# Sixteen keys in 128 rows: zero-filled last blocks in a two-layer attention and retention kernel

## The chip, the cores and the metric

The kernel runs on one core of a Trainium2 chip. The metric is the device time of one execution in microseconds (us). Three runs of the kernel before took 1307.19, 1303.7 and 1307.78 us; their median is 1307.19 us. One further execution was taken with the hardware profiler: it took 1307.29 us, and its trace spans 1305.5 us.

## What is computed

The model is a trunk of two layers. Each layer normalises its input, projects it once, splits the columns into a softmax attention with forget gates (8 heads of 64, called FoX here) and a retention (4 heads of 128), joins both, projects back, and runs a gated feed-forward network. 16 learned "meta" tokens stand ahead of the 512 real tokens, so the sequence has 528 positions: four blocks of 128 and a last one of 16.

```python
def fox_attention(q, k, v, logf):
    ...
    def attend(q_blk, c_q, q_pos, k_, v_, c_k, k_pos):
        s = jnp.einsum('bhqd,bhkd->bhqk', q_blk, k_).astype(jnp.float32) * scale
        s = s + c_q[..., :, None] - c_k[..., None, :]
        s = jnp.where(k_pos[None, :] <= q_pos[:, None], s, -jnp.inf)
        p = jax.nn.softmax(s, axis=-1)
        return jnp.einsum('bhqk,bhkd->bhqd', p.astype(v_.dtype), v_)
...
def retention_chunkwise(q, k, v):
    """o_t = sum_{s<=t} gamma_h^(t-s) (q_t.k_s) v_s."""
...
def hybrid_layer(h, ...):
    xn = rmsnorm(h, attn_norm_g)
    proj = jnp.einsum('bld,dc->blc', xn, w_in)
    ...
    mix = jnp.concatenate([fox_out, ret_out], axis=-1)
    h = h + jnp.einsum('blc,cd->bld', mix, w_out)
    ...
    return h + jnp.einsum('blf,fd->bld', ff, w_down)
```

## The kernel before

Activations lie transposed, features on the 128 partitions and the 528 positions along the free dimension. Every product is made in float32r with both operands split into a high and a low part (`split`, L119: ScalarE copies the high part, VectorE subtracts it to get the low part), so that a product is two or three matmuls. In the trace such tiles come in pairs: `pth` and `ptl`, `rsh` and `rsl`, `rvh` and `rvl`, `whi` and `wlo`.

A layer has two stages. In the attention stage (the pool `att`, entered by `enter_att`, L81) the dense projections of w_in and w_out run on TensorE (L191), and the steps of the attentions are placed between them. In the feed-forward stage (the pool `ffn`) there are only dense products and forms of them (L803, L938). The two pools lie over each other: a tile of a pool waits for the tile of the earlier pool on whose addresses it lies.

The order of TensorE is written out by hand: `layer` builds a list of steps, `merge` (L215) puts each attention step at a given place between the dense steps, and `tc.manual_schedule` (L1121) keeps TensorE in that order. The other engines' order is left to a scheduler. Weights arrive by DMAs of SyncE's queue (L135); ScalarE copies their high part (`whi`, L167), and VectorE or GpSimd subtracts the low part (`wlo`, L168).

The attention steps that the change touches:

- `transpose_into` (L369) transposes column blocks of a tile on TensorE, up to four into one PSUM bank. It takes `parts`, the number of rows of its source, and `last`, the number of columns in a last block that stands alone. Its matmul (L378) has the data as the stationary operand, which a weight load brings into the array, and an identity matrix (`idt`) as the moving one.
- FoX (`fox_steps`, L425; two heads share a step list, s = 0 and 1). `values` (L431) transposes V in five blocks at `KOFF`, the last of 16 columns, and splits it into `vv`. `scores` (L447) makes the logits of one query block and writes the exponentials to `p_tiles[b]`, or, for the 16 meta queries, to one of two tiles of 16 rows (`pm_tiles`). `turn` (L497) transposes them into `pth` and `ptl`, [128, 5, 528]; for meta queries the source has 16 rows (`nq`). `product` (L507) multiplies by the values: five key blocks, a high and a low matmul for each, all in one PSUM bank. The fifth block has `KLEN[4]` = 16 rows of both operands and only 16 queries.
- Retention (`ret_steps`, L592). `values` (L598) transposes `vr`, subtracts the mean over each head's 128 columns and splits into `rvh` and `rvl`. `scores` (L617) makes the decayed products of key blocks; the blocks 2, 3 and 4 share a pair of tiles `rsh` and `rsl`, and the part of block 4, 16 rows by 16 columns, is split by itself (L651). `product` (L654) takes three matmuls for a block (high by high, high by low, low by high), for the fifth block with 16 rows.
- Layer 0 also computes the 16 meta queries, layer 1 doesn't. So a run has 16 FoX products (8 heads, 2 layers), 8 retention products, and 8 transposes of meta queries.

The rows of a matmul are the partitions of both its operands, over which it sums. The lines at which the fifth block gets its 16 rows:

```python
rows = last if j0 + len(grp) == len(offs) and len(grp) == 1 else 128
nc.tensor.transpose(ps[0:rows, 128 * j:128 * j + parts], src[:, o:o + rows], idt[0:parts, 0:parts])
...
kn = KLEN[j]
nc.tensor.matmul(po[:, c0:SEQ], v[0:kn, j, :], pp[0:kn, j, META + c0:T],
                 start=(j == 0 and i == 0), stop=(j == 4 and i == 1))
```

Of the kernel before, what the change touches and what calls it, by code (L numbers as in the profile page):

```python
# [17 lines left out]
SEQ = 512  # L18
# [20 lines left out]
def hybrid_kernel(ctx, tc, x_t, w_in, w_fl, w_out, w_gate, w_up, w_down, vecs, b_fg, rope, decay, mask, ident, out_t):  # L39
# [24 lines left out]
    onec = const.tile([128, 1], F32, name="onec")  # L64
    nc.vector.memset(onec, 1.0)

    p_tiles, pm_tiles, vt_tiles, low_keys = [], [], [], []
    rot = {"pm": 0, "vt": 0}


    phase = {}
# [9 lines left out]
    def enter_att(l):  # L81
        enter("att")
        low_keys[:] = [phase["att"].tile([128, T], F32R, name=f"kl{s}") for s in range(2)]
        for s, t in enumerate(low_keys):
            (nc.gpsimd if l else nc.vector).memset(t[64 * (1 - s):64 * (2 - s)].bitcast(F32), 0.0)
        for lst, n, shape in ((p_tiles, NBLK, [128, TP]), (pm_tiles, 2, [META, 128]), (vt_tiles, 1, [128, T])):
            lst[:] = [phase["att"].tile(shape, F32, name=f"pd{shape[1]}_{n}_{i}") for i in range(n)]

            for i, t in enumerate(lst):
                if lst is not vt_tiles:  # L90
                    z0 = META + 128 * (i + 1) if lst is p_tiles else META
                    (nc.gpsimd if l else nc.vector).memset(t[:, z0:z0 + 128 - META], 0.0)

    def take(lst, key):
        t = lst[rot[key] % len(lst)]
# [273 lines left out]
    def transpose_into(src, offs, parts=128, last=128):  # L369


        out = []
        for j0 in range(0, len(offs), 4):
            grp = offs[j0:j0 + 4]
            ps = psum_a()
            rows = last if j0 + len(grp) == len(offs) and len(grp) == 1 else 128
            for j, o in enumerate(grp):
                nc.tensor.transpose(ps[0:rows, 128 * j:128 * j + parts], src[:, o:o + rows], idt[0:parts, 0:parts])  # L378
            out.append((j0, len(grp), rows, ps[0:rows, 0:128 * len(grp)].rearrange("p (j q) -> p j q", j=len(grp))))
        return out  # L380

    def fox_dense(l, g, ly, real, st):
# [28 lines left out]
                st["k"].append((kh, kl))  # L411

        def v_done(ps):
            vt = take(vt_tiles, "vt")
# [10 lines left out]
    def fox_steps(g, st, ly, real):  # L425
# [21 lines left out]
        def scores(s, b):  # L447
# [11 lines left out]
            for c0, c1 in segs:  # L459
                sc = psum_a()  # L460
                for i, kk in enumerate(st["k"][s]):
                    nc.tensor.matmul(sc[0:nq, 0:c1 - c0], st["q"][s][:, q0:q0 + nq], kk[:, c0:c1],  # L462
                                     start=(i == 0), stop=(i == 1))
                if c1 == nk:
                    diag = sc[0:nq, c1 - c0 - nq:c1 - c0]
                    nc.vector.tensor_add(diag, diag, msk[0:nq, 0:nq])
                nm = tmp.tile([128, 1], F32, name="nmax", tag="nmax", bufs=6)
                nc.vector.tensor_tensor_reduce(pt[:, c0:c1], sc[0:nq, 0:c1 - c0], bc[0:nq, c0:c1],  # L468
                                               -1.0, 3.0e38, ALU.add, ALU.min, nm[0:nq])
                mins.append(nm)  # L470
            nmax = mins[0]
# [8 lines left out]
            pr = pt[:, 0:nk]  # L480
# [16 lines left out]
        def turn(s, b):  # L497
            nq, nk, q0 = span(b)
            if b == blocks[0]:
                st["pt"] = (at("pth", shape=(128, 5, T)), at("ptl", shape=(128, 5, T)))  # L500
            pth, ptl = st["pt"]
            if (s, b) == todo[-2]:
                normalise()
            for j0, n, _, p3 in transpose_into(info[s, b], [128 * j for j in range(b + 2)], nq):
                split(pth[:, j0:j0 + n, q0:q0 + nq], ptl[:, j0:j0 + n, q0:q0 + nq], p3[:, :, 0:nq])

        def product(s):  # L507
# [10 lines left out]
            po = psum_a()  # L518
            for j in range(5):
                c0 = max(0, KOFF[j] - META)  # L520
                kn = KLEN[j]
                for i, pp in enumerate(pt):
                    nc.tensor.matmul(po[:, c0:SEQ], v[0:kn, j, :], pp[0:kn, j, META + c0:T],  # L523
                                     start=(j == 0 and i == 0), stop=(j == 4 and i == 1))
            nc.scalar.copy(ol[a0:a1, META:T], po[b0:b1, :])
            nc.vector.tensor_add(mt[a0:a1, META:T], po[a0:a1, :], ol[a0:a1, META:T])
# [30 lines left out]
    def ret_dense(l, hd, ly, real, st, which):  # L557
# [34 lines left out]
    def ret_steps(l, hd, st, real):  # L592
# [5 lines left out]
        def values():  # L598
            vh = at("rvh", shape=(128, 5, 128))
            vl = at("rvl", shape=(128, 5, 128))  # L600
            mean = tmp.tile([128, 5, 1], F32, name="mean", tag="mean")
            for j0, n, rows, p3 in transpose_into(st["vr"], KOFF, last=META):
                mn = mean[0:rows, j0:j0 + n]
                nc.vector.tensor_reduce(mn, p3, axis=mybir.AxisListType.X, op=ALU.add)
                nc.vector.tensor_scalar_mul(mn, mn, -1.0 / 128.0)
                for j in range(n):
                    nc.scalar.activation(vh[0:rows, j0 + j], p3[:, j], AF.Identity, bias=mn[:, j])
                for j in range(n):
                    nc.vector.scalar_tensor_tensor(vl[0:rows, j0 + j], p3[:, j], mn[:, j],
                                                   vh[0:rows, j0 + j].bitcast(F32), ALU.add, ALU.subtract)  # L610
            st["rv"] = (vh, vl)

        def q_start(j):
# [3 lines left out]
        def scores(grp):  # L617
# [30 lines left out]
            full = used if kn == 128 else used - n  # L648
            split(sh[:, 0:full], sl[:, 0:full], sd[:, 0:full])
            if full < used:  # L650
                split(sh[0:kn, full:used], sl[0:kn, full:used], sd[0:kn, full:used])  # L651
            kept["t", grp[0]] = (sh, sl)

        def product(grp):  # L654
# [4 lines left out]
            po, d = st["po"], st["d"]  # L659
            for j in grp:  # L660
                used, g0 = kept[j]
                sh, sl = kept["t", g0]
                q0 = q_start(j)
                qa = max(q0, META)
                kn = KLEN[j]
                for i, (a, b) in enumerate(((vh, sh), (vh, sl), (vl, sh))):
                    nc.tensor.matmul(po[:, qa - META:SEQ], a[0:kn, j, :], b[0:kn, used + qa - q0:used + T - q0],  # L667
                                     start=(j == 0 and i == 0), stop=(j == 4 and i == 2))
                if j == 0 and not real:
                    pm = psum_a()  # L670
# [525 lines left out]
```

## Time and profile before

| | before |
|---|---|
| median of three runs | 1307.19 us (1303.7 to 1307.78) |
| profiled execution | 1307.29 us |
| its span in the trace | 1305.5 us |
| TensorE matmul, busy | 1274.1 us, 98% of the span, 9326 matmuls |
| TensorE weight loads, busy | 1210.3 us, 93% |
| VectorE busy | 1009.4 us, 77% |
| ScalarE busy | 705.4 us, 54% |
| GpSimd busy | 195.4 us, 15% |

In the rows of the profile, PE is TensorE's matmul side, PEld its weight loads, DVE VectorE, ACT ScalarE, POOL GpSimd and SP SyncE. A row names the source line, the engine, the operation and the tiles (out<-in). A matmul's form reads rows*columns of the stationary operand, then the shape of the output: `16*128 16x16` has 16 rows in the array. In a timeline the first column is the start in us from the span's start, the second the time that the merged instructions (x2, x4) cover. A matmul's end is modelled and includes time in which it waits in the array, so starts say more than durations: what a matmul costs in a stream is the distance to the next start.

### The profile page before, as it was taken

What the parts mean: (1) busy time and instruction counts of PE and PEld (TensorE: products, weight loads), DVE (VectorE), ACT (ScalarE), POOL (GpSimd) and SP (SyncE); (2) the same over time, 40 slices, a digit from 0 to 9 for tenths busy, and PEclk for the clock granted to TensorE, in tenths of its full rate; (3) what the DMA queues carried; (4) which work ended last, traced back from release to release, by engine and by line L of the source; (5) the groups of instructions that cost most, each with busy time, mean ns of one, the idle gap of its engine ahead of it and who ended that gap; (6) DMA issues with size and microseconds to landing.
All of it is one profiled execution on the core that took longest, in us unless ns stands there. A gap on an engine that the chain in (4) does not pass through costs nothing.

```text
span 1305.5 us, 23282 instructions
## 1 busy us (share of the span) xinstructions
PE 1274.1 (98%) x9326; PEld 1210.3 (93%) x9326; DVE 1009.4 (77%) x1823; ACT 705.4 (54%) x1276; POOL 195.4 (15%) x153
## 2 busy tenths in 40 slices
PE   8999999999999999999999999999999999999996
PEld 7999999999999999999998989988779999999995
DVE  7877756879888887777786777567799887888866
ACT  6766645667444444444466665456664444444444
POOL 3332433230000000000013324333200000000000
PEclk9999999999999999999999999999999999999998
DMA  5322222213233333332323222222223333333321
GB/s 195 107 66 82 74 82 82 64 59 126 77 122 98 97 98 98 98 98 81 99 73 114 74 69 95 83 80 63 92 85 104 127 98 97 98 98 99 112 66 65
DMA packets 45468, 120.54 MB, mean 92 GB/s; under 512 B 5376, under 2 KB 12032, under 8 KB 45360
## 3 DMA queue, kind: packets, MB, share of 16 engines
q1 hardware_dynamic: 45120, 118.90, 28.8%
q8 instruction: 73, 1.20, 0.4%
q0 software_dynamic: 96, 0.13, 0.1%
q14 instruction: 35, 0.29, 0.1%
q10 hardware_dynamic: 144, 0.02, 0.0%
HBM read 116.91 MB, written 2.13 MB: 91 GB/s over the span
## 4 chain that ended last, share of the span: by engine, by line
PE 80%; DVE 12%; ACT 5%; issue 1%; DMA 1%; POOL 0%; SPq 0%; DVEq 0%; ACTq 0%; POOLq 0%
PE psd L191 21%; PE psa L803 18%; PE psd L938 13%; PE psd L803 13%; PE psa L938 4%; PE psa L191 3%; PE psa L378 2%; PE psa L523 1%; DVE xl L284 1%; PE psa L667 1%; PE psa L462 1%; PE psa L640 1%; DVE ss L299 1%; DVE wlo L168 1%; ACT whi L167 1%
## 5 line engine op out<-in xcount | busy, mean ns | idle before, releaser
L168 POOL TENSOR_TENSOR wlo<-raw,whi 128x512 fp32r<-128x512 f32 x136 | 189.7, 1411 | 398.9 <-ACT whi L167 396.4
L191 PE MATMUL psd<-xh,whi 128*128 128x264 f32 (+1 forms) x792 | 198.6, 319 | 8.8 <-ACT whi L167 4.9
L191 PE MATMUL psd<-xh,wlo 128*128 128x264 f32 (+1 forms) x792 | 188.0, 305 | 0.4 <-POOL wlo L168 0.4
L191 PE MATMUL psd<-xl,whi 128*128 128x264 f32 (+1 forms) x792 | 187.7, 304 | 0.0
L191 PEld LDWEIGHTS psd<-xh,whi 128*128 128x128 f32 x792 | 129.9, 192 | 14.6 <-ACT whi L167 6.7
L191 PEld LDWEIGHTS psd<-xh,wlo 128*128 128x128 f32 x792 | 128.4, 190 | 6.4 <-POOL wlo L168 0.6
L191 PEld LDWEIGHTS psd<-xl,whi 128*128 128x128 f32 x792 | 129.1, 191 | 4.2 <-DVE xl L284 0.3
L167 ACT CAST whi<-raw 128x512 fp32r<-128x512 f32 (+1 forms) x170 | 99.4, 613 | 43.9 <-PE psd L191 20.5
L791 ACT CAST whi<-raw 128x1024 fp32r<-128x1024 f32 (+2 forms) x62 | 54.9, 885 | 51.9 <-PE psd L803 38.9
L791 ACT CAST fwhi<-raw 128x1024 fp32r<-128x1024 f32 (+2 forms) x62 | 55.7, 899 | 47.4 <-PE psd L803 39.9
L792 DVE TENSOR_TENSOR wlo<-raw,whi 128x1024 fp32r<-128x1024 f32 (+2 forms) x62 | 62.9, 1015 | 11.7 <-ACT whi L791 11.6
L792 DVE TENSOR_TENSOR fwlo<-raw,fwhi 128x1024 fp32r<-128x1024 f32 (+2 forms) x62 | 64.0, 1032 | 8.8 <-ACT fwhi L791 8.7
L481 ACT ACTIVATE pd<-pd,nmax 128x144 f32<-128x144 f32 (+4 forms) x72 | 39.3, 545 | 53.0 <-DVE nmax L468 40.4
L803 PE MATMUL psa<-tl,whi 128*128 128x264 f32 (+1 forms) x232 | 65.8, 284 | 0.0
L803 PE MATMUL psa<-th,whi 128*128 128x264 f32 (+1 forms) x232 | 65.8, 284 | 0.0
L803 PE MATMUL psa<-th,wlo 128*128 128x264 f32 (+1 forms) x232 | 65.6, 283 | 0.0
L121 DVE TENSOR_TENSOR ptl<-psa,pth 128x512 fp32r<-128x512 f32 (+4 forms) x88 | 42.0, 491 | 28.0 <-ACT pth L120 27.6
L803 PE MATMUL psa<-th,fwhi 128*128 128x264 f32 (+1 forms) x224 | 63.6, 284 | 0.0
L803 PE MATMUL psa<-th,fwlo 128*128 128x264 f32 (+1 forms) x224 | 63.5, 283 | 0.0
L803 PE MATMUL psa<-tl,fwhi 128*128 128x264 f32 (+1 forms) x224 | 63.4, 283 | 0.0
L869 ACT COPY e<-psa 128x264 f32<-128x264 f32 (+1 forms) x114 | 42.9, 376 | 28.6 <-PE psa L803 24.5
L791 ACT CAST fwhi<-S 128x1024 fp32r<-128x1024 f32 x20 | 21.0, 1050 | 68.1 <-PE psa L803 66.3
(290 smaller groups left out, 4031.7 us busy)
## 6 DMA issues: line engine op xcount, KB each, us to landing
raw<-w_in SPq DMA_DIRECT2D x54, 512.0 KB, 3.5
raw<-w_gate SPq DMA_DIRECT2D x44, 512.0 KB, 3.9
fraw<-w_up SPq DMA_DIRECT2D x38, 512.0 KB, 3.5
raw<-w_down SPq DMA_DIRECT2D x64, 256.0 KB, 2.9
raw<-w_out SPq DMA_DIRECT2D x16, 512.0 KB, 3.4
raw<-w_down SPq DMA_DIRECT2D x32, 192.0 KB, 2.4
bc<-cdr SPq DMA_DIRECT2D x16, 264.0 KB, 3.4
raw<-w_up SPq DMA_DIRECT2D x6, 512.0 KB, 3.4
```

Source lines behind the costliest of these rows:

```text
L121: nc.vector.tensor_sub(lo, src, hi.bitcast(F32))
L167: nc.scalar.copy(hi, job["raw"][:, c0:c1])
L168: sub(lo, job["raw"][:, c0:c1], hi.bitcast(F32))
L191: nc.tensor.matmul(ps[1][b][:, 0:c1 - c0], w[:, wk, :], x[:, c0:c1], start=(k == 0 and i == 0), stop=(k == n - 1 and i == 2))
L284: nc.vector.scalar_tensor_tensor(xl[:, c], h[k][:, c], g, xh[:, c].bitcast(F32), ALU.mult, ALU.subtract)
L378: nc.tensor.transpose(ps[0:rows, 128 * j:128 * j + parts], src[:, o:o + rows], idt[0:parts, 0:parts])
L481: nc.scalar.activation(pr, pr, AF.Exp, bias=nmax[0:nq], scale=-1.0, accum_out=rsum)
L791: nc.scalar.copy(hi, src)
L792: nc.vector.tensor_sub(lo, src, hi.bitcast(F32))
L803: nc.tensor.matmul(bank()[:, 0:w], a[:, o + k, :], b, start=(fresh and k == 0 and i == 0), stop=(k == n - 1 and i == 2), skip_group_check= ...
L869: nc.scalar.copy(self.t["e"][:, i], self.t["x"][:, 0:w])
L938: nc.tensor.matmul(v[:, 0:c1 - c0], a[:, s * n + k, :], b[:, c0:c1], start=(k == 0 and i == 0), stop=(k == n - 1 and i == 2))
```

## The change

The last block of 16 keys, and the 16 meta queries that are transposed, get 128 rows, of which 112 hold zeros.

- `enter_att` makes two tiles of 640 columns for V (`v_tiles`, one for each attention), whose last 112 columns are set to zero, instead of a `vt` tile of 528 columns and the later tile `vr`; two `pm_tiles` of 128 rows instead of 16, set to zero entirely, in layer 0 only; and four tiles of 16 columns (`end_tiles`) for the retention's last block, set to zero.
- `transpose_into` always transposes 128 rows and 128 columns.
- Both `values` take 128 rows of the last block, zeros in 112 of them, and both `product`s sum over 128 rows. In the retention the split of block 4's 16 by 16 part goes to a pair of `end_tiles` instead of the end of `rsh` and `rsl`.

```diff
+        for lst, n, cols, z0 in ((p_tiles, NBLK, TP, None), (v_tiles, 2, TP, T)):
+            lst[:] = [phase["att"].tile([128, cols], F32, name=f"pd{z0}_{i}") for i in range(n)]
             for i, t in enumerate(lst):
...
+                z = META + 128 * (i + 1) if z0 is None else z0
+                zero(l, t[:, z:z + 128 - META])
+        pm_tiles[:] = [phase["att"].tile([128, 128], F32, name=f"pm{i}") for i in range(2)] if l == 0 else []
+        for t in pm_tiles:
+            zero(l, t)
+        end_tiles[:] = [[phase["att"].tile([128, META], F32R, name=f"rs{i}{k}") for k in range(2)] for i in range(2)]
+        for t in end_tiles[0] + end_tiles[1]:
+            zero(l, t.bitcast(F32))
+
+    def zero(l, t):
+        (nc.gpsimd if l else nc.vector).memset(t, 0.0)
...
-                nc.tensor.transpose(ps[0:rows, 128 * j:128 * j + parts], src[:, o:o + rows], idt[0:parts, 0:parts])
+                nc.tensor.transpose(ps[:, 128 * j:128 * j + 128], src[:, o:o + 128], idt)
...
-            for j0, n, rows, p3 in transpose_into(st["vt"], KOFF, last=META):
+            for j0, n, p3 in transpose_into(st["vt"], KOFF):
                 for s in range(2):
-                    v = st["v"][s][0:rows, j0:j0 + n]
+                    v = st["v"][s][:, j0:j0 + n]
...
-            for j0, n, _, p3 in transpose_into(info[s, b], [128 * j for j in range(b + 2)], nq):
+            for j0, n, p3 in transpose_into(info[s, b], [128 * j for j in range(b + 2)]):
...
-                    nc.tensor.matmul(po[:, c0:SEQ], v[0:kn, j, :], pp[0:kn, j, META + c0:T],
+                    nc.tensor.matmul(po[:, c0:SEQ], v[:, j, :], pp[:, j, META + c0:T],
                                      start=(j == 0 and i == 0), stop=(j == 4 and i == 1))
...
-            vr = at("vr", F32)
+            vr = v_tiles[1]
...
             if full < used:
-                split(sh[0:kn, full:used], sl[0:kn, full:used], sd[0:kn, full:used])
+                eh, el = end_tiles[hd % 2]
+                split(eh[0:kn], el[0:kn], sd[0:kn, full:used])
+                kept["e"] = (eh, el)
...
+                if j == 4:
+                    (sh, sl), used = kept["e"], 0
                 for i, (a, b) in enumerate(((vh, sh), (vh, sl), (vl, sh))):
-                    nc.tensor.matmul(po[:, qa - META:SEQ], a[0:kn, j, :], b[0:kn, used + qa - q0:used + T - q0],
+                    nc.tensor.matmul(po[:, qa - META:SEQ], a[:, j, :], b[:, used + qa - q0:used + T - q0],
                                      start=(j == 0 and i == 0), stop=(j == 4 and i == 2))
```

In the built program each engine issues the same instructions in the same order as before, with these exceptions: VectorE has six more memsets at the start of layer 0 and GpSimd four more at the start of layer 1; two small scalings of gain vectors on VectorE come four places later at the start; and in two places the 16 by 16 split of the retention's last block stands three or four places earlier on ScalarE and VectorE. SyncE's queue of DMAs is the same.

More of the change, by code (lines that the diff above doesn't have):

```diff
@@ L65, in hybrid_kernel @@
     nc.vector.memset(onec, 1.0)
-    p_tiles, pm_tiles, vt_tiles, low_keys = [], [], [], []
-    rot = {"pm": 0, "vt": 0}
+    p_tiles, pm_tiles, v_tiles, end_tiles, low_keys = [], [], [], [], []
+    rot = {"pm": 0}
     phase = {}
@@ L367, in silu, with transpose_into @@
             tc.keep_in_program_order(nc.scalar.preload_act_table_set("natural_log_exp_and_others"))
-    def transpose_into(src, offs, parts=128, last=128):
+    def transpose_into(src, offs):
         out = []
@@ L375, in transpose_into @@
             ps = psum_a()
-            rows = last if j0 + len(grp) == len(offs) and len(grp) == 1 else 128
             for j, o in enumerate(grp):
-                nc.tensor.transpose(ps[0:rows, 128 * j:128 * j + parts], src[:, o:o + rows], idt[0:parts, 0:parts])
-            out.append((j0, len(grp), rows, ps[0:rows, 0:128 * len(grp)].rearrange("p (j q) -> p j q", j=len(grp))))
+                nc.tensor.transpose(ps[:, 128 * j:128 * j + 128], src[:, o:o + 128], idt)
+            out.append((j0, len(grp), ps[:, 0:128 * len(grp)].rearrange("p (j q) -> p j q", j=len(grp))))
         return out
@@ L413, in v_done @@
         def v_done(ps):
-            vt = take(vt_tiles, "vt")
+            vt = v_tiles[0]
             for t, (c0, c1) in zip(ps, FULL):
@@ L601, in values @@
             mean = tmp.tile([128, 5, 1], F32, name="mean", tag="mean")
-            for j0, n, rows, p3 in transpose_into(st["vr"], KOFF, last=META):
-                mn = mean[0:rows, j0:j0 + n]
+            for j0, n, p3 in transpose_into(st["vr"], KOFF):
+                mn = mean[:, j0:j0 + n]
                 nc.vector.tensor_reduce(mn, p3, axis=mybir.AxisListType.X, op=ALU.add)
```

19 lines of the change are left out of this document (6 added, 13 removed).

## The prediction

> **What bounds the kernel now.** I read the page first, its busy times and its chain of work, then the chain in order of time.
>
> ```profile
> PE 1274.1 (98%) x9326; PEld 1210.3 (93%) x9326; DVE 1009.4 (77%) x1823; ACT 705.4 (54%) x1276; POOL 195.4 (15%) x153
> PE 80%; DVE 12%; ACT 5%; issue 1%; DMA 1%; POOL 0%; SPq 0%; DVEq 0%; ACTq 0%; POOLq 0%
> ```
>
> TensorE is busy for 98% of the span and carries 80% of the chain, so a slot that falls away on it usually shortens the run. The reader should see the other 20% too: there are stretches in the attention stages where the chain leaves TensorE. These rows of the chain (start, length, what) are the first piece off TensorE and the first piece back on it, for the five stretches that will matter:
>
> ```profile
> 106.04 0.69 DVE mean L604
> ...
> 133.17 0.72 PE psa L667 x2
> ...
> 684.58 1.79 POOL wlo L168
> ...
> 723.89 0.99 PE psa L640 x9
> ...
> 761.84 0.48 ACT pth L120
> ...
> 780.05 0.74 PE psa L667 x2
> ...
> 886.84 0.17 ACT pth L120
> ...
> 901.89 0.76 PE psa L378 x5
> ...
> 907.39 0.76 ACT pth L120 x2
> ...
> 919.09 0.50 PE psa L259
> ```
>
> Between these pairs VectorE and ScalarE hand work to each other and TensorE waits at the end; what TensorE saves inside them is lost.
>
> **The gap round a matmul of 16 rows.** Next I read the weight loads in order of time, because in a stream of short matmuls the distance from load to load is the price. Here are the end of a FoX product (fourth block, then the two matmuls of 16 rows, then a dense product), and three matmuls with the shape that the change gives these: 16 columns moved, 128 rows.
>
> ```profile
> 61.10 0.19 PEld L523 LDWEIGHTS psa<-ptl,vv 128*128 128x128 f32 x1
> 61.36 0.18 PEld L523 LDWEIGHTS psa<-pth,vv 16*128 16x128 f32 x1
> 61.47 0.18 PEld L523 LDWEIGHTS psa<-ptl,vv 16*128 16x128 f32 x1
> 61.67 0.30 PEld L191 LDWEIGHTS psd<-xh,whi 128*128 128x128 f32 x2
> ```
>
> ```profile
> 73.84 0.19 PEld L672 LDWEIGHTS psa<-rsl,rvh 128*128 128x128 f32 x1
> 73.95 0.19 PEld L672 LDWEIGHTS psa<-rsh,rvl 128*128 128x128 f32 x1
> 74.06 0.30 PEld L191 LDWEIGHTS psd<-xh,whi 128*128 128x128 f32 x2
> ```
>
> With 128 rows each load follows the one before by 0.11 us. With 16 rows the step into the pair is 0.26, inside it 0.11, out of it 0.20. So the array pays some 0.15 us on the way in and 0.10 on the way out, as if it ran empty when the number of rows changes, and the rows themselves make no load shorter (0.18 against 0.19).
>
> Two pages of the Trainium skill part here. "TensorE: Matmul & The Clock Gate", section "LDWEIGHTS (loading the stationary operand)", has a load's time depend on columns alone, not on rows; by that the change would save nothing, and it speaks against it. "TensorEngine Tiling (Array Packing)", section "Key Properties", says that "Changing tiling mode (not just tile) drains the TensorE". The trace agrees with the first on durations (0.18 and 0.19) and with the second on distances (0.26 and 0.20 against 0.11). The first becomes a rival below.
>
> **The change part by part.** How many FoX products and meta transposes there are:
>
> ```profile
> L378 PE MATMUL psa<-idt,pd 16*128 16x16 f32 x8 | 1.8, 230 | 0.0
> L523 PE MATMUL psa<-pth,vv 16*128 16x16 f32 x16 | 4.4, 272 | 0.0
> ```
>
> FoX products, 16. From 61.10 to 61.67 is 0.57 us; three steps of 0.11 are 0.33: 0.24 to 0.25 us saved where a dense product follows. In the eight second heads the four transposes of the sums follow (L531):
>
> ```profile
> 79.64 0.20 PEld L531 LDWEIGHTS psa<-idt,tq 128*128 128x128 f32 x2
> ```
>
> Two loads of 0.14 in 0.20: the second comes only 0.06 after the first, not 0.11, so 0.05 is given back already and 0.20 is left. Eight of each: 8 x 0.25 + 8 x 0.20 = 3.6 us.
>
> Retention products, 8 (four heads, two layers), with three matmuls of 16 rows each:
>
> ```profile
> 82.64 0.19 PEld L667 LDWEIGHTS psa<-rsh,rvl 128*128 128x128 f32 x1
> ...
> 83.33 0.30 PEld L191 LDWEIGHTS psd<-xh,whi 128*128 128x128 f32 x2
> ```
>
> From 82.64 to 83.33 is 0.69, four steps of 0.11 are 0.44: 0.25 saved, 8 x 0.25 = 2.0 us.
>
> Transposes of meta queries, 8. Before, and (second fence) a group of full transposes behind the same kind of dense pair:
>
> ```profile
> 45.43 0.31 PEld L191 LDWEIGHTS psd<-xh,wlo 128*128 128x128 f32 x2
> 45.88 0.14 PEld L378 LDWEIGHTS psa<-idt,pd 16*128 16x128 f32 x1
> 46.05 0.30 PEld L191 LDWEIGHTS psd<-xh,whi 128*128 128x128 f32 x2
> ```
>
> ```profile
> 74.54 0.31 PEld L191 LDWEIGHTS psd<-xh,wlo 128*128 128x128 f32 x2
> 74.80 0.58 PEld L378 LDWEIGHTS psa<-idt,pd 128*128 128x128 f32 x5
> ```
>
> From the dense pair to the next one it is 0.62 us now. A full transpose starts 0.26 after the pair and takes a step of 0.11 (five in 0.58): 0.37. So 0.25 is saved, although it is now larger: 8 x 0.25 = 2.0 us.
>
> Transposes of the values' last block, 16 groups of five. The columns of the stationary operand go from 16 to 128:
>
> ```profile
> 41.06 0.53 PEld L378 LDWEIGHTS psa<-idt,pd 128*128 128x128 f32 x5
> ```
>
> The fifth of these five, the short one, starts 0.44 after the first (0.53 less its own 0.09), at the same step of 0.11; it is the moving identity that is long, and it stays. I take 0; the bounds are 0 and 16 x 0.05 = 0.8 us of loss, if 0.14 instead of 0.09 showed.
>
> ScalarE and VectorE on the last block go from 16 partitions to 128 with the same columns:
>
> ```profile
> L607 ACT ACTIVATE rvh<-psa,mean 128x128 fp32r<-128x128 f32 x32 | 9.2, 370 | 9.4 <-DVE mean L605 9.3
> L607 ACT ACTIVATE rvh<-psa,mean 16x128 fp32r<-16x128 f32 x8 | 2.7, 343 | 0.0
> ```
>
> 27 ns eight times, 0.2 us, off TensorE: 0. The 16 by 16 split has the same size and another target. That it stands three or four places earlier in two places puts one such split each ahead of work that TensorE awaits: bounds 0 and 2 x 0.2 us.
>
> Memsets. At the start VectorE does this, and the chain does that:
>
> ```profile
> 3.90 0.28 DVE L92 MEMSET pd<- 16x112 f32 x2
> ...
> 4.55 0.77 DVE L284 SCALAR_TENSOR_TENSOR xl<-h,vec,xh 128x528 fp32r<-128x528 f32 x1 [0.30 <-ACT xh L283]
> ```
>
> ```profile
> 2.13 5.40 DMA h<-x_t
> ```
>
> Six more at 0.14 each end at 3.90 + 0.28 + 0.84 = 5.02, so `xl` could come 0.47 us late, and TensorE's second matmul group behind it. The cover is the load of the second `h`, which lands at 7.53 and sets the chain: 0, and 0.5 us without that cover. GpSimd, busy for 15% of the span, takes four more at the start of layer 1, before any step that reads them: 0. No wait on a DMA is added, and SyncE's queue keeps its order.
>
> So TensorE's gross saving is 3.6 + 2.0 + 2.0 = 7.6 us. Seven of the 32 places lie inside the five stretches off TensorE, the first and the last of them:
>
> ```profile
> 120.01 0.27 PE L523 MATMUL psa<-pth,vv 16*128 16x16 f32 x1
> 915.05 0.27 PE L667 MATMUL psa<-rsh,rvh 16*128 16x16 f32 x1
> ```
>
> They are FoX products at 120.0, 713.1, 769.5, 892.8 and 910.9, a meta transpose at 122.0 and a retention product at 915.1: 4 x 0.25 + 0.20 + 0.25 + 0.25 = 1.7 us. Net 7.6 - 1.7 = 5.9. The profiled execution took 1307.29 (1.79 outside its span) and stands 0.1 over the median of the three runs, so the forecast is 1307.3 - 5.9 = 1301.4 us.
>
> **The rivals.**
>
> 1. Nothing is gained: the distances belong to matmuls of 16 columns or to the weight load, not to the rows (this is where the rule on loads leads). Time 1307.3. Against it stand the three matmuls at 73.84, as short, with 128 rows and no gap; for it only that the shape has not been seen behind a block of 144 columns.
>
> 2. VectorE takes the gain back: with 77% of the span it has some slack, but in the attention stages single VectorE results release TensorE, and TensorE that comes earlier waits longer there. If half the net gain goes that way, the time is 1307.3 - 3.0 = 1304.3. For it: five such stretches exist already. Against: outside them the chain is on TensorE for tens of us at a time, and VectorE's inputs come from TensorE, so they move up too.
>
> 3. Slower, by collisions of VectorE with GpSimd. The same two subtractions of the retention's scores take, without and with a GpSimd subtraction beside them:
>
> ```profile
> 268.76 0.67 DVE L121 TENSOR_TENSOR rsl<-sd,rsh 128x416 fp32r<-128x416 f32 x2 [1.15 <-ACT rsh L120]
> 137.66 1.42 DVE L121 TENSOR_TENSOR rsl<-sd,rsh 128x416 fp32r<-128x416 f32 x2 [0.19 <-ACT rsh L120]
> ...
> 137.26 1.29 POOL L168 TENSOR_TENSOR wlo<-raw,whi 128x512 fp32r<-128x512 f32 x1 [2.74 <-ACT whi L167]
> ```
>
> That is 0.75 us a collision. "GPSIMD Engine Reference", section "Specifications", of the Trainium skill has the two engines share their SBUF interfaces, which agrees. The place is the five stretches, where VectorE sets the end. When TensorE runs earlier, GpSimd's subtractions shift against VectorE's; with 14 more collisions on the chain, 10.5 us, the run is 10.5 - 5.9 = 4.6 slower: 1311.9. It turns to a loss from the eighth on. As many may fall away as are added, which speaks against it.
>
> **How the numbers follow.** Chances: the forecast 0.68, rival 1 0.08, rival 2 0.18, rival 3 0.06. About 0.3%, 3.9 us, is what a measurement of this kernel can tell from no change: below 1303.3 is faster, above 1311.1 slower. The forecast's own range: all 7.6 us seen gives 1299.7; the unknown costs (0.8, 0.4, 0.5) give 1303.1. The three runs of before lie up to 3.5 below their median, so I take 2 more on the lower side: 1297.7. Upward, 1305.5 takes in rival 2 with 1.2 for the runs. Rivals 1 and 3 stay out, 0.14. Faster: 0.95 of the forecast and 0.3 of rival 2, 0.70. Slower: most of rival 3, 0.05. Same: 0.25.
>
> **What would show it.** In the changed profile no matmul or weight load has 16 rows; loads at the end of both products follow each other by 0.11, and from the dense pair over a meta transpose to the next pair it is 0.37 instead of 0.62. TensorE's idle time inside the five stretches grows by about 1.7 us in all. Steps that stay at 0.20 and more at the ends of products prove rival 1; shorter products with as much more waiting for VectorE prove rival 2; more VectorE operations of double length on the chain prove rival 3. The forecast is wrong if the gap at these places goes and the time does not fall by at least 4 us.

## The result and the profile after

| | before | after |
|---|---|---|
| median (runs) | 1307.12 us (8) | 1302.65 us (8) |
| lowest to highest | 1303.7 to 1308.37 | 1301.95 to 1304.6 |
| profiled execution, its span | 1307.29, 1305.5 us | 1302.06, 1300.3 us |
| TensorE matmul, busy | 1274.1 us | 1267.2 us |
| idle time of TensorE at waits for `sql` (head norms) | 0.2 us, once | 0.6 us, three times |

After over before is 0.9971, 95% interval 0.9962 to 0.998: 4.5 us by the medians, 2.6 to 5.0 by the interval. A second set of runs of the same kernel (below) gave 0.9977, 0.9967 to 0.9987, and 3.6 us by the medians. The forecast had 5.9 us, which lies above both intervals (2.6 to 5.0 and 1.7 to 4.3 us).

The changed code stands some lines lower in its file: L191 is now L199, L259 L267, L378 L384, L523 L528, L667 L675, L739 L747. From the page of the changed kernel, the busy times and the engines' shares of the chain:

```profile
PE 1267.2 (97%) x9326; PEld 1205.1 (93%) x9326; DVE 1010.7 (78%) x1829; ACT 705.5 (54%) x1276; POOL 195.1 (15%) x157
...
PE 76%; DVE 14%; ACT 7%; issue 2%; DMA 1%; POOL 0%; SPq 0%; DVEq 0%; ACTq 0%; POOLq 0%
```

The number of matmuls is the same, TensorE is busy for 6.9 us less, and the chain has left it for another 4% of the span: more of the chain lies on VectorE and ScalarE. The place of the prediction's second view, the end of a FoX product, in the timeline of weight loads of the changed kernel (start and length in us, then the row):

```profile
59.15 0.19 PEld L528 LDWEIGHTS psa<-ptl,vv 128*128 128x128 f32 x1
59.26 0.19 PEld L528 LDWEIGHTS psa<-pth,vv 128*128 128x128 f32 x1
59.41 0.19 PEld L528 LDWEIGHTS psa<-ptl,vv 128*128 128x128 f32 x1
59.52 0.30 PEld L199 LDWEIGHTS psd<-xh,whi 128*128 128x128 f32 x2
```

And a transpose of meta queries between two dense pairs:

```profile
43.74 0.31 PEld L199 LDWEIGHTS psd<-xh,wlo 128*128 128x128 f32 x2
44.00 0.14 PEld L384 LDWEIGHTS psa<-idt,pm 128*128 128x128 f32 x1
44.11 0.30 PEld L199 LDWEIGHTS psd<-xh,whi 128*128 128x128 f32 x2
```

The steps 0.26, 0.11 and 0.20 at the product have become 0.11, 0.15 and 0.11, so this first product saved 0.20; the sum over all sixteen follows below. The 0.62 us over the meta transpose have become 0.37, as forecast.

Both kernels give TensorE 9326 matmuls in the same order, so the n-th start of one trace can be set against the n-th of the other. What a stretch gained or lost is how much that distance moved over it. This table is worked out that way, before against after, and holds all that the difference is made of:

| | places | us |
|---|---|---|
| ends of FoX products | 16 | -3.67 |
| ends of retention products | 8 | -1.95 |
| transposes of meta queries | 8 | -1.97 |
| given back inside the five stretches: 0.52 (122 to 138), 0.26 (714 to 727), 0.19 (770 to 784), 0.27 (893 to 902), 0.49 (918) | 5 | +1.73 |
| given back at head norms (L259) at 87, 275, 735 and 793 us | 4 | +1.68 |
| given back at FoX scores at 252 us | 1 | +0.49 |
| the rest, none over 0.05 | | -0.1 |
| the change | | -3.8 |
| the start up to 45 us (full speed from 8.3 us on instead of 13.3, and the second load of `h` lands at 6.87 instead of 7.53) and the granted clock (a half-speed stretch of 3.4 us at 320 us missing; one of 3.4 us more at 896 us) | | -1.4 |

The last row is put down to chance: two profiles of the unchanged kernel before differ by 1.2 us at the start and by 1.4 at 320 us (next section). The profiled executions are 5.2 us apart, and 3.8 of these belong to the change. Two profiles of one kernel also differ by up to 0.17 us between 640 and 901 us, so tenths in this table aren't sharp.

One of the norms, that of head 0 in layer 0, in the two timelines. Before:

```profile
83.13 0.69 DVE L532 TENSOR_TENSOR mixt<-psa,mixt 128x512 f32<-128x512 f32 x1
...
83.85 0.63 ACT L120 CAST mxh<-mixt 128x528 fp32r<-128x528 f32 x1 [3.01 <-DVE mixt L532]
...
85.00 0.65 ACT L677 ACTIVATE sq<-d 128x528 f32<-128x528 f32 x1
...
86.35 0.71 DVE L121 TENSOR_TENSOR sql<-sq,sqh 128x528 fp32r<-128x528 f32 x1
...
87.06 0.41 PE L259 MATMUL psa<-sqh,ones 128*128 128x264 f32 x2
...
87.30 0.40 PE L259 MATMUL psa<-sql,ones 128*128 128x264 f32 x2
```

After:

```profile
80.75 0.69 DVE L537 TENSOR_TENSOR mixt<-psa,mixt 128x512 f32<-128x512 f32 x1
...
81.47 0.64 ACT L128 CAST mxh<-mixt 128x528 fp32r<-128x528 f32 x1 [3.02 <-DVE mixt L537]
...
82.62 0.65 ACT L685 ACTIVATE sq<-d 128x528 f32<-128x528 f32 x1
...
83.97 0.71 DVE L129 TENSOR_TENSOR sql<-sq,sqh 128x528 fp32r<-128x528 f32 x1
...
84.17 0.41 PE L267 MATMUL psa<-sqh,ones 128*128 128x264 f32 x2
...
84.73 0.51 PE L267 MATMUL psa<-sql,ones 128*128 128x264 f32 x2 [0.16 <-DVE sql L129]
```

TensorE reaches the first matmul 2.89 us earlier, but the square starts only 2.38 earlier, and its low part ends at 84.68 instead of 87.06. The retention's product, which the square is made from, isn't what holds it: that ends 2.8 us earlier. ScalarE stands ahead of the square with the cast `mxh`, for which it waits 3 us for VectorE's `mixt`, and VectorE, which has worked almost without pause since 76 us, comes to `mixt` 2.38 us earlier. Before, the low part ended 0.24 ahead of the matmul that reads it; now that matmul waits for it, and over this norm 0.43 is lost.

### The profile page after: what moved, and what is told of

It is laid out like the page before. It is cut to its first block, busy times and chain, and to the rows that moved or that the text cites. A ratio compares the mean times of both kernels' runs of the same rounds, so it can differ in the third digit from the quotient of the medians.

```text
span 1300.3 us, 23291 instructions
## 1 busy us (share of the span) xinstructions
PE 1267.2 (97%) x9326; PEld 1205.1 (93%) x9326; DVE 1010.7 (78%) x1829; ACT 705.5 (54%) x1276; POOL 195.1 (15%) x157
## 4 chain that ended last, share of the span: by engine, by line
PE 76%; DVE 14%; ACT 7%; issue 2%; DMA 1%; POOL 0%; SPq 0%; DVEq 0%; ACTq 0%; POOLq 0%
PE psd L199 18%; PE psa L811 18%; PE psd L946 13%; PE psd L811 13%; PE psa L946 4%; PE psa L199 3%; PE psa L384 2%; DVE xl L292 1%; PE psa L468 1%; ACT whi L175 1%; DVE ss L307 1%; PE psa L528 1%; DVE wlo L176 1%; DVE tq L573 1%; PE psa L645 1%
## 5 line engine op out<-in xcount | busy, mean ns | idle before, releaser
L199 PE MATMUL psd<-xh,whi 128*128 128x264 f32 (+1 forms) x792 | 197.4, 317 | 8.5 <-ACT whi L175 4.9
L199 PE MATMUL psd<-xh,wlo 128*128 128x264 f32 (+1 forms) x792 | 187.2, 304 | 0.4 <-POOL wlo L176 0.4
L199 PE MATMUL psd<-xl,whi 128*128 128x264 f32 (+1 forms) x792 | 187.1, 304 | 0.2 <-DVE xl L292 0.2
L199 PEld LDWEIGHTS psd<-xh,whi 128*128 128x128 f32 x792 | 128.8, 190 | 13.2 <-ACT whi L175 6.7
L199 PEld LDWEIGHTS psd<-xh,wlo 128*128 128x128 f32 x792 | 127.5, 189 | 6.6 <-POOL wlo L176 0.6
L199 PEld LDWEIGHTS psd<-xl,whi 128*128 128x128 f32 x792 | 128.1, 189 | 4.8 <-DVE xl L292 0.9
L487 ACT ACTIVATE pdNone<-pdNone,nmax 128x144 f32<-128x144 f32 (+1 forms) x64 | 37.0, 577 | 48.3 <-DVE nmax L474 36.0
```

The source lines that it names most:

```text
L199: nc.tensor.matmul(ps[1][b][:, 0:c1 - c0], w[:, wk, :], x[:, c0:c1], start=(k == 0 and i == 0), stop=(k == n - 1 and i == 2))
```

## The experiments

**Which numbers of rows open the gap.** In the changed kernel, the last block of the products cut to a number of rows for each place (the rows left out hold zeros):

```diff
-                    nc.tensor.matmul(po[:, c0:SEQ], v[:, j, :], pp[:, j, META + c0:T],
+                    nc.tensor.matmul(po[:, c0:SEQ], v[0:kn, j, :], pp[0:kn, j, META + c0:T],
...
+                kn = (32, 64)[s] if j == 4 else 128
...
-                    nc.tensor.matmul(po[:, qa - META:SEQ], a[:, j, :], b[:, used + qa - q0:used + T - q0],
+                    nc.tensor.matmul(po[:, qa - META:SEQ], a[0:kn, j, :], b[0:kn, used + qa - q0:used + T - q0],
...
+                kn = (96, 16, 32, 64)[hd] if j == 4 else 128
```

> The changed kernel with the fifth block of the products cut again, to a different number of rows in each place: FoX products 32 rows in the first head of a pair and 64 in the second, retention products 96, 16, 32 and 64 rows in heads 0 to 3. The rows left out are zeros, so nothing else changes. Theory (the gap comes from a change of the number of rows): the load of the first short matmul follows the block before by 0.26 us wherever the count differs from 128, the load after the last short one follows by 0.20, and inside the group 0.11; 96 rows behave either like 64 (any change counts) or like 128 (only whole parts of the array count), which the theory leaves open. Rival A (only the 16 rows, by their small number, are slow): 32, 64 and 96 rows show 0.11 throughout. Rival B (the gap belongs to the load that is started behind a block with more columns): all counts, 128 too, would show it, which the changed kernel's profile speaks against. Time by the theory: FoX 16 places and 7 of 8 retention places back, about 3.2 us over the changed kernel if what was given back is the same share as there (1305.5); by rival A 1302.5.

One run, 1307.24 us. Weight loads of this kernel at the end of a FoX product with 32 rows, of one with 64, and of a retention product with 96:

```profile
59.58 0.19 PEld L529 LDWEIGHTS psa<-ptl,vv 128*128 128x128 f32 x1
59.84 0.18 PEld L529 LDWEIGHTS psa<-pth,vv 32*128 32x128 f32 x1
59.95 0.18 PEld L529 LDWEIGHTS psa<-ptl,vv 32*128 32x128 f32 x1
60.15 0.30 PEld L199 LDWEIGHTS psd<-xh,whi 128*128 128x128 f32 x2
...
77.28 0.19 PEld L529 LDWEIGHTS psa<-ptl,vv 128*128 128x128 f32 x1
77.54 0.18 PEld L529 LDWEIGHTS psa<-pth,vv 64*128 64x128 f32 x1
77.65 0.19 PEld L529 LDWEIGHTS psa<-ptl,vv 64*128 64x128 f32 x1
77.86 0.31 PEld L537 LDWEIGHTS psa<-idt,tq 128*128 128x128 f32 x3
...
80.84 0.19 PEld L677 LDWEIGHTS psa<-rsh,rvl 128*128 128x128 f32 x1
80.95 0.30 PEld L677 LDWEIGHTS psa<-rs,rvh 96*128 96x128 f32 x2
81.18 0.19 PEld L677 LDWEIGHTS psa<-rs,rvl 96*128 96x128 f32 x1
81.29 0.30 PEld L199 LDWEIGHTS psd<-xh,whi 128*128 128x128 f32 x2
```

With 32 and with 64 rows the steps are those of 16 rows: 0.26 or 0.27 in, 0.11 inside, 0.20 or 0.21 out, in all 16 FoX products and in the six retention products with 16, 32 and 64 rows. With 96 rows they are those of 128, 0.11 throughout, in both products of that head. Rivals A and B fall. It isn't any change of the number of rows that costs: 16, 32 and 64 stand on one side, 96 and 128 on the other. The time is 1.7 us over the theory's 1305.5; TensorE ran at half speed for 6.8 us at 898 us in this execution, and one run can't tell whether that is all of it.

**The price by itself.** One matmul of zeros more, 16 columns moved, in the feed-forward stages of the changed kernel, where TensorE waits for next to nothing; once with 16 rows, once with 128:

```diff
+                        if k == 1 and i == 0:
+                            nc.tensor.matmul(bank()[:, 0:META], a[0:16, o + k, :], zr[0:16, :],
+                                             start=False, stop=False, skip_group_check=True)
```

> The changed kernel with one more matmul in each of the 190 half-row products of the feed-forward stages, at their second step: 16 columns of zeros, 16 rows, added to the sum that is there. It adds nothing to the result. TensorE waits for next to nothing in these stages, so the price of a place is seen whole. Theory (0.26 into a short matmul of fewer rows, 0.20 out of it, against one step of 0.11 before): 0.35 us a place, 66 us in all, 1369. Rival A (the weight load sets the price, whatever the rows): 0.11 a place, 21 us, 1323, the same as with 128 rows. Rival B (in a stream of long matmuls the gap hides behind the matmul before it): the same 1323 with 16 rows, but 0.26 where short matmuls are neighbours.

> The same 190 matmuls of zeros with 128 rows instead of 16. All theories: one more load step of 0.11 us a place, 21 us, 1323. The difference to the kernel with 16 rows is the price of the change of rows alone: by the theory 0.25 a place, 47 us; by both rivals 0.

Medians of two runs: 1415.98 us with 16 rows, 1335.83 with 128. The matmul stands in 282 products and not in 190 (the groups of its rows count 86, 82, 58 and 56), so the totals are larger than expected: 33.2 us more than the changed kernel's 1302.65 with 128 rows, 0.118 a place, and 80.2 more than that with 16, 0.284 a place. (The kernel before took 1307.08 us beside these two and 1307.12 beside the changed one, so the first difference can be read as well.) Both rivals, which had the two kernels alike, fall. Weight loads of both, 16 rows first:

```profile
431.08 0.19 PEld L813 LDWEIGHTS psa<-th,fwhi 128*128 128x128 f32 x1
431.41 0.18 PEld L816 LDWEIGHTS psa<-zr,fwhi 16*128 16x128 f32 x1
431.61 0.19 PEld L813 LDWEIGHTS psa<-tl,fwhi 128*128 128x128 f32 x1
```

```profile
421.13 0.19 PEld L813 LDWEIGHTS psa<-th,fwhi 128*128 128x128 f32 x1
421.26 0.19 PEld L816 LDWEIGHTS psa<-zr,fwhi 128*128 128x128 f32 x1
421.38 0.19 PEld L813 LDWEIGHTS psa<-tl,fwhi 128*128 128x128 f32 x1
```

The step out is 0.20 here too. The step in is 0.33 behind a matmul of 264 columns, and 0.26 behind one of 144. That fits an array that has to finish the matmul before it, but no row shows this. So the gap doesn't hide behind the matmul before it, it is the larger one behind the longer of the two lengths measured, and where TensorE waits for next to nothing it reaches the end: 0.53 against 0.25 from load to load in these rows is 0.28, as in the times.

**The parts alone.** The change in the meta transposes alone (`kn = 16` for the last block of both products), and in the products alone (the meta transposes take `src[0:16]` and `idt[0:16, 0:16]`):

> The change in the transposes of the meta queries alone: these take 128 rows and columns, the last block of both products has 16 rows as before the change. Theory: from the dense pair over the meta transpose to the next dense pair 0.37 us instead of 0.62, ends of products 0.26 and 0.20 as before; gross 2.0, 7 of 8 places on TensorE's path 1.75; with the share kept by the whole change (4.1 of 7.6) 1.1 us faster than before, 1306.0; by the sum on record 1305.4. Rival (the meta transposes carry the gain, since nothing waits behind them): 2.0 or more faster, 1305 or less, and the products alone nearly nothing.

> The change in the two products alone: their last block has 128 rows, the transposes of the meta queries stay at 16 rows and 16 columns. Theory (each place saves its own gap, what lies before a late VectorE result is given back): the steps at the ends of products are 0.11, those round a meta transpose 0.26 and 0.17 as before. Gross 3.6 + 2.0 = 5.6 us; with the share that the whole change kept (4.1 of 7.6) 3.0 us faster than before, 1303.1 against the 1306.1 that the kernel before showed beside the transposes alone. By the sum on record (1.45 given back in five stretches) 4.15 faster, 1302.0. Rival (nothing is kept where VectorE follows: the products end in VectorE and ScalarE work, the meta transposes do not): under 1.5 us faster, above 1304.6.

| | median (runs) | to before | gained at its places | kept by 310 us, layer 0 | kept 640 to 901 us, layer 1 |
|---|---|---|---|---|---|
| meta transposes alone | 1305.87 (10) | 0.9992, 0.9983 to 1.0002 | 1.96 | 1.34 | -0.27, has no place there |
| products alone | 1304.77 (10) | 0.9982, 0.9973 to 0.9991 | 5.63 | 1.48 | 0.56 |
| both (the change) | 1302.65 (8) | 0.9971, 0.9962 to 0.998 | 7.59 | 2.96 | 0.77 |

The last three columns compare starts with the kernel before, one by one, from 45 us on. In layer 0 the parts add up: 1.34 and 1.48 are 2.82 of 2.96. In layer 1 they can't be told that finely: against the second profile of the kernel before (below) the three figures are -0.10, 0.73 and 0.94. Both give back a share, the products more. Of the 4.15 us that the sum on record has for the products, the interval (1.2 to 3.5 us) excludes the whole. The rival for them, under 1.5 us, isn't excluded by the interval, but the starts have 2.0; that for the transposes, 2.0 or more, falls by the starts with 1.3, while the interval (0.3 slower to 2.2 faster) tells neither it nor a gain from nothing.

**Where the granted clock falls.** The kernels before and after once more, unchanged:

> The kernel before, unchanged, in one more profile. Theory (the stretches of a few us in which the granted clock stands at half are not bound to an instruction, so part of the difference between the two profiles is not the change): the stretch at the start ends at another time than 13.0 us, or the one at 320 us is missing or has another place or length, by 1 us or more of TensorE's time; steps at the places of the change stay at 0.26 and 0.20. Rival (they are set by the work, so the kernel before always has them there): the same ends and lengths within 0.2 us.

> The changed kernel, unchanged, on the same chip as the next two. Theory (the change itself is worth about 4.1 us, read from the places of the two traces; the rest of the first difference of 4.5 is where the granted clock fell): 3.5 to 4.8 us faster than before. Rival (the sum on record, 5.9): 5.4 or more. A stretch of half clock follows a period of 3.41 us in which TensorE idled 1.9 us or more, and no other; the rival there is that it stands at 320 us or 895 us whatever the idle time in the period before.

Before: one run, 1304.6 us; every step at the 32 places is the same within 0.01, full speed began at 10.6 us, and there was no half-speed stretch at 320 us. By the starts it was 2.6 us ahead of the first profile at the end: 1.2 from the first 45 us, where the second load of `h` also landed 0.9 us earlier, and 1.4 from 320 us. After: 1303.69 us (8 runs), 0.9977 with an interval of 0.9967 to 0.9987, 3.6 us, so the theory holds and the rival of 5.4 or more falls; the clock had both stretches, at 317 and at 897 us, behind steps with 2.2 and 3.0 us of idle time, and the gain at the places was 7.56.

Busy times in stretches of 3.41 us, counted in such steps from the start of full speed (columns: us, then PE, PEld, DVE, ACT and POOL busy, then the granted clock). First profile of before:

```profile
317.07:320.48 3.41, 1.50 (x13) 1.29 (x11) 3.41 (x7) 2.96 (x5) 0.00 (x0) 1.00 0.46 154
320.48:323.89 3.41, 3.09 (x14) 3.12 (x15) 3.41 (x8) 0.97 (x2) 0.00 (x0) 0.50 0.09 18
```

Second profile of before:

```profile
314.34:317.75 3.41, 2.91 (x25) 2.70 (x23) 3.41 (x7) 2.93 (x6) 0.00 (x0) 1.00 0.20 43
317.75:321.16 3.41, 1.72 (x14) 1.75 (x15) 3.41 (x7) 2.37 (x3) 0.00 (x0) 1.00 0.27 111
321.16:324.57 3.41, 3.41 (x30) 3.41 (x30) 3.41 (x8) 1.80 (x3) 0.00 (x0) 1.00 0.36 115
```

The wait for `sg` is 2.2 us in both. In the first, 1.91 of it lies in one step, and the next step runs at half speed; in the second it is cut into 0.50 and 1.69, and nothing happens. The page "TensorE: Matmul & The Clock Gate" of the Trainium skill, in its section "🔬 Part 1: The HAM clock gate (the "warmup" mystery)", has such a window run freely, without regard to the kernel; the traces agree (3.413 us, and starts of full speed from 7.8 to 13.3 us). Its table has the half clock come after at least one idle window; here 1.91 us of one were enough. So where the half-speed stretches fall in the table of the result is taken for chance.

**Whether TensorE's order can take back what was given back.** The head norms of heads 0 to 2 two dense steps later:

```diff
-            m0, r0, places = (((7, 31), (34, 40.5), (13, 33.5, 35.5, 37.5, 39, 40.5, 43, 44, 47.5, 48)),
-                              ((0.5, 31.5), (32, 40), (13, 33.5, 35.5, 37.5, 39, 41, 43, 44, 47.5, 48)))[g]
+            m0, r0, places = (((7, 31), (34, 40.5), (13, 33.5, 35.5, 37.5, 39, 40.5, 43, 44, 49.5, 50)),
+                              ((0.5, 31.5), (32, 40), (13, 33.5, 35.5, 37.5, 39, 41, 43, 44, 49.5, 50)))[g]
...
-                      ret_places(2, 26, 22.5, 23.5, 32, 28, 33.5, 36, 56.5, 40.5, 57.5),
+                      ret_places(2, 26, 22.5, 23.5, 32, 28, 33.5, 36, 56.5, 42.5, 57.5),
```

> The changed kernel with the head norms of the retention heads 0, 1 and 2 two dense steps later in TensorE's order (position 47.5 to 49.5, 40.5 to 42.5; the gates of heads 0 and 1 move with them), and nothing else. Theory (part of the gain is given back because TensorE reaches the norm before VectorE has the square's low part): the waits of the norm's matmuls for sqh and sql in the middle of the two attention stages go, four times 0.2 to 0.4 us, and the kernel is about 1.0 us faster than the changed one, 1301.6 against its 1302.65. Rival (VectorE as a whole has no slack there, so the wait only moves to its next result): the same total of TensorE's waits in the attention stages, 1302.65 within 0.5.

1301.9 us (5 runs), 0.9958, 0.9944 to 0.9972. The waits at the norms of heads 0 and 1 are gone (0.8 us together), and a wait of 0.6 us at 248 us stands where one of 0.35 was. The time agrees with the theory, but the interval takes in the changed kernel's ratio, so the runs don't tell the two apart. By the starts it kept 0.7 us more than the changed kernel in layer 1 and nothing more in layer 0. Next, the largest wait near the changed places, the values of head 3 (`ret_places(3, 50, ...` becomes `53`), alone and with all norms:

> The changed kernel with the transposes of the values of the last retention head three dense steps later in TensorE's order (position 50 to 53). In both traces TensorE waits 2.7 and 3.0 us for these values in layer 1, and behind the wait of the changed kernel the clock stands at half for 3.4 us. Theory (the wait is a matter of TensorE's order, and dense steps that are ready can fill it): the wait falls under 1 us, the half-clock stretch behind it goes, and the time falls by 2 to 4.5 us against the changed kernel. Rival (VectorE is behind with everything there, as the chain has it from 887 to 902 us): TensorE only waits at the next place, for the scores or the products of the same head, and the time stays within 1 us.

> The changed kernel with the values of the last retention head three steps later, the head norms of heads 0 to 2 two steps later and that of head 3 behind the gate's dense group (63 to 64.05). Theory: the waits of the norms for sqh and sql in the attention stages fall from about 2.1 us to under 0.5, which adds 1 to 1.5 us to what the later values bring: 3 to 6 us faster than the changed kernel. Rival (VectorE has no slack): no faster than the later values alone.

1302.29 us (5 runs; 0.9962, 0.9949 to 0.9976) and 1304.0 us (6 runs; 0.9971, 0.996 to 0.9983), beside 1303.69 for the changed kernel on the same chip. From the waits of the later values (what TensorE waited for, total, times, longest), where the changed kernel has 3.0 us for `pd`:

```profile
PE psa L675 <- DVE rvl L614: 2.6, 2, 1.5
```

The half-speed stretch at 896 us went, but the wait came back in front of the first product, in both layers: 1.4 us faster is neither the theory's 2 or more nor the rival's 1 or less, but the wait went where the rival has it. With all norms late the waits went to the gates of the dense products behind them (`mxh`, 1.8 us). Last, the norms of heads 0 and 1, and the values and products of head 3 in layer 1 only, once with the change and once with the short blocks of 16 rows put back:

```diff
-                      ret_places(3, 50, 45.5, 47.5, 55.5, 55.5, 56.5, 58.5, 64.1, 63, 64.2))
+                      ret_places(3, *((53, 45.5, 47.5, 56.5, 56.5, 57, 59) if real else
+                                      (50, 45.5, 47.5, 55.5, 55.5, 56.5, 58.5)), 64.1, 63, 64.2))
```

> The changed kernel with three of the moves alone: the head norms of heads 0 and 1 two dense steps later, and, in layer 1 only, the values of head 3 three steps later with its first product behind the last FoX product (55.5 to 56.5, the second 56.5 to 57, the third 58.5 to 59). Theory (these waits are a matter of TensorE's order): the norms' waits at 84, 729 and 786 us stay away as they did with the late norms (0.8 us together), the 1.6 us that the later values left in front of the first product is covered by the FoX product, and no half-clock stretch stands at 895 us: 3 to 5 us faster than the changed kernel, ratio to before 0.994 to 0.996, and faster than both kernels. Rival (VectorE is the limit at the end of the attention stage): the wait moves to the last products or to the norm of head 3, and the gain over the changed kernel is 1 us or less.

> The same moves with the short last blocks put back: 16 rows in both products and in the transposes of the meta queries. Theory (what the change gave back outside the five stretches went to waits of TensorE at head norms, scores and transposes that its order sets): compared place by place with the kernel before it, the change now gives back nothing at the norms of heads 0 and 1 (0.7 us less than between the kernels before and after), so it is worth about 4.8 us instead of 4.1. Rival (VectorE's rate sets the end of each attention stage, whatever the order): what was not given back at the norms is given back at the next wait, and the change is worth 4.1 us or less here too.

1303.29 us (8 runs; 0.9977, 0.9967 to 0.9988) and 1310.03 us (10 runs; 1.0024, 1.0015 to 1.0034). In the waits of the first of them:

```profile
PE psa L528 <- DVE rvl L614: 1.5, 1, 1.5
```

As a faster kernel, it misses: the wait for `rvl` only moved to the FoX product (L528), and no version here is shown to be faster than the changed one. As a test of the cause it answers. Between these two kernels nothing is given back at the norms of heads 0 and 1 (0.04 at most, against 1.26 at the same three places before), 0.22 of it goes to the stretch at 131 us (0.74 instead of 0.52), and by 901 us the change has kept 4.93 us instead of 3.73. The theory had 0.7 more; it is 1.2: 0.95 more in layer 1 (1.72 against 0.77) and 0.25 more in layer 0 (3.21 against 2.96), where about half of what the norm gained went to the next wait, as the rival has it. The rival's 4.1 or less falls. The medians are 6.7 us apart, more than that. In the profiled executions, 9.2 apart, the kernel with 16 rows had two half-speed stretches more, at 908 and 918 us; whether these make up the rest of the medians isn't shown.

## Why the forecast was too large

The time, 1302.65 us, came out 1.25 over the forecast and inside its range; the saving didn't reach the 5.9. Point by point, by the steps of the prediction.

- What bounds the kernel: right, 97% after 98%, and the matmuls that lost their gap became a gain.
- The gap and its cause: right. The load itself is as long as before (0.19), the distances shrank, and rival 1 falls with that. The page "TensorEngine Tiling (Array Packing)" of the Trainium skill, section "Key Properties", has a change of tiling mode drain TensorE. The runs with 32, 64 and 96 rows and the longer step behind a longer matmul fit that; the drain itself isn't seen in any row. The prediction's "when the number of rows changes" was too wide: 96 next to 128 costs nothing.
- The gross sum: 7.6 forecast, 7.59 measured. FoX products 3.67 (3.6: the eight ahead of the transposes of the sums saved 0.22 each and not 0.20), retention 1.95 (2.0), meta transposes 1.97 (2.0).
- What was costed at nothing: no step of TensorE behind the transposes of the values is longer, and no wait on the zeros was added. The six memsets at the start cost nothing either. They fill the time in which VectorE waited for `xh`, and the first `xl` starts at 4.54 us after 4.55, not 0.47 late (rows of the changed kernel); the two scalings of `gn` that stood there come later:

```profile
4.16 0.30 DVE L100 MEMSET pm<- 128x128 f32 x2
4.41 0.14 DVE L100 MEMSET rs<- 128x16 f32 x4
4.54 0.77 DVE L292 SCALAR_TENSOR_TENSOR xl<-h,vec,xh 128x528 fp32r<-128x528 f32 x1
```

- The five stretches: 1.7 forecast, 1.73 measured, and not by luck in the sum: 0.50, 0.25, 0.25, 0.25 and 0.45 forecast, 0.52, 0.26, 0.19, 0.27 and 0.49 measured.
- The step that failed is the one against rival 2, "outside them the chain is on TensorE for tens of us at a time, and VectorE's inputs come from TensorE, so they move up too". Being on TensorE says that a wait there is zero, not how far from zero it is. At four head norms and one group of scores the VectorE result that TensorE needs was ready only 0.08 to 0.31 us ahead before the change, and it moved up by less than TensorE did: by 2.38 us against 2.89 at the norm shown, by 4.68 against 5.17 at the scores at 252 us, where it is a `ptl`. VectorE has its inputs from TensorE, but at the norm shown it was behind: it took up `mixt` (L532, at 83.13) 2.8 us after TensorE's transposes that this reads had ended. 2.2 us more went to these places, and the net was 3.8 instead of 5.9. With later norms in TensorE's order the change kept 1.2 us more, so this cause is shown for the norms of heads 0 and 1; for the other norm and the scores it was only read.
- Rival 2 has the mechanism that the five further places show. Of the net it had half go, 3.0 kept; the 3.8 that is left of the change lies nearer to that than to 5.9.
- That the time came as near to the forecast as it did is in part luck: 1307.3 less the 3.8 of the change is 1303.5, and the median of the result lay 0.85 below that. By the prediction's own sign, a fall of at least 4 us, the first set of runs (4.5) passes, the second (3.6) and the starts (3.8) don't.
- Rival 3: the profiles have no sign of it. VectorE was busy for 1010.7 us after 1009.4. Its instructions that took over 1.4 times the median of their shape (and over 0.3 us) number 58 and 59 in the two profiles before, 60 and 60 in the two after; the loss would have needed eight more on the chain.

## What to carry over

In a stream of short matmuls read the distance from load to load, not the duration of one: the gap of 0.25 to 0.28 us at a block of few rows showed in no duration, and filling the block with zeros to the full height removed it at no cost that the traces show. When TensorE saves time at many places, sum what comes before the next operand that another engine makes, and ask at each such place by how much the operand is early, even where the profile shows no wait. Compare the starts of two traces one by one before believing a difference of medians: here a quarter of what the two profiles differed by was the start and the clock.

## What the hardware showed that was not expected

Matmuls of 64 rows pay the same gap as those of 16 (0.26 or 0.27 us in, 0.20 or 0.21 out), those of 96 rows none (0.11 and 0.11).

The granted clock falls to half for a whole 3.41 us step when TensorE idled long enough in the step before, and the steps begin at no fixed place of the kernel. Over the 14 profiled executions told of here, with steps counted from the start of full speed: all 19 steps with 2.1 us or more of idle time were followed by half speed, 10 of 13 with 1.85 to 2.1, and 4 of some 5270 with less. So the same wait of 2.2 us cost 1.4 to 1.5 us more in some executions (at 320 us, between two profiles of one kernel) and nothing in others, which may be a part of the 3 to 5 us by which runs of one kernel differ. This is worked out from the traces and not tested with a kernel made for it.
